# A decoder layer on eight cores: dealing out the query chunks evenly, and reworking how weights arrive before the first mixer

## The chip, the cores and the metric

One Trainium2 chip, all eight cores (dies: cores 0 to 3 and 4 to 7), one launch. The metric is device microseconds of the slowest core. On this chip an execution of such a program falls into one of two states: fast, where the granted TensorE clock averages about 0.96 to 0.98 on every core, or slow, where the cores of one die or both get less. "TensorE", "DVE", "ACT" and "Pool" are the matrix, vector, scalar and GpSimd engines; the rows of a profile name them PE (PEld for its weight loads), DVE, ACT and POOL, and SPq is the queue of plain DMAs.

## The reference, cut to what matters

```python
# x: (4, 4096, 2048); 8 heads of 128
h = rmsnorm(x)                       # then q, k, v, u, two gates = split(h @ w_in)
y_attn = stick_breaking_attention(q, k, v) @ w_attn_branch     # strictly causal
y_pool = (grouped(trailing_means(u, (2, 4, 8, 16)) - u) * pool_scale) @ w_pool_branch
x = x + rmsnorm((sigmoid(g_attn) * y_attn + sigmoid(g_pool) * y_pool) @ w_out)
up = causal_depthwise_conv(rmsnorm(x) @ w_up, width=3)         # 2 x 5632 channels
x = x + rmsnorm((gelu(gate) * val) @ w_down)
x = x + rmsnorm(sigmoid(x @ w_ple_gate) * (p @ w_ple))
```

Two cores share a sequence of 4096 tokens, that is 8 chunks of 512. Cores do not exchange anything: each makes keys and values for all chunks it attends to, and everything else for its own four chunks.

## The kernel before: the parts that matter

A core owned one half of a sequence. All eight run one program, so the program is the one of the second half, and cores with the first half ran it on zeros in front:

```python
xa = x[b] if half == 1 else np.concatenate([np.zeros((2048, D)), x[b, :2048]], axis=0)
...
groups = [(h, cc) for h in range(NH) for cc in range(c, -1, -1)]   # c = 4 + t, t = 0..3
```

So query chunk t goes over 5 + t key chunks. One step ("unit") takes 128 queries and 512 keys of one head: a score matmul, a sigmoid on ACT, a scan on DVE, four transposes, a copy on ACT, a weighted sum. Attention is interleaved with other TensorE work: the first one with the projections of chunks 5 to 7, the other three with mixers 0 to 2.

Weights come in float32. A DMA on the Pool queue can cast. Most units (0.5 MB in bf16) are first converted in DRAM, two at a time, and read from there through a ring of eight slots:

```python
def convert(u0, u1):                                  # float32 wst -> bf16 ws, DRAM to DRAM
    P.dma("pool", s_cv, [(ws[u0:u1]..., wst[u0:u1]...)], writes=[("ws", u0, u1)])
...
conv.extend(range(U_V, U_UP, 2))                      # 44 pairs: V, Q and all mixer weights
kst = [alloc(NT, BF16) for _ in range(3)]             # staging of K and Q on their way to DRAM
```

A helper works out, for every instruction, the semaphores it has to wait on; a conversion reads and writes DRAM only, so it waits for nothing but its place in the Pool queue.

## Time and profile before

| | before |
|---|---|
| four runs | 4899.15, 4901.73, 4919.94, 5198.72 us |
| profiled run, slowest core | 4903.9 us |
| TensorE busy | 4356.2 us (89%), union of matmul spans |
| start to first mixer | 1110 us |
| first to last mixer (attention beside) | 1326 us |
| last mixer, up, rest | 277, 647, 1544 us |

How to read it: from the first mixer on TensorE has little idle time, so there only a smaller count of matmuls helps. The first 1110 us are different. A busy total is not the amount of work: a 512-column matmul has a span of about 380 ns, but one can start every 215 ns.

### The profile page before, as it was taken

To read this page: it belongs to the slowest core of one execution; us is meant where nothing else is said; L and a number is where in the kernel's file an instruction comes from. 1 tells how busy PE (TensorE), PEld (TensorE's weight loads), DVE (VectorE), ACT (ScalarE), POOL (GpSimd) and SP (SyncE) were. 2 spreads that over 40 slices of the span, in tenths; PEclk is the share of its full clock that TensorE was granted. 3 is DMA by queue.
4 is the path that set the end of the run, shared out by engine and by line. 5 is a ranking of instruction groups with operands and counts; after the bars stand their busy time and mean duration, and the time that the engine had idled before them with its cause. 6 is when DMAs were issued, how large, how long until landed. Compare 5 with 4: busy or idle time off the path is not lost.

```text
span 4903.9 us, 73190 instructions; the slowest of 8 cores (4867.4 to 4903.9 us)
## 1 busy us (share of the span) xinstructions
PE 4356.2 (89%) x25253; PEld 2306.8 (47%) x25664; DVE 2274.5 (46%) x2149; ACT 1846.1 (38%) x3066; POOL 289.6 (6%) x652
## 2 busy tenths in 40 slices
PE   5896371899998999899799899999999999999988
PEld 2343130456864454455444566665444444444444
DVE  2221110696766887888531544442215444402244
ACT  2221010585555666666521333332003333301144
POOL 1000000000000000100000111110001111000000
PEclk9998685999999999999999999999999999999999
DMA  9799879554444544544553988886665444347643
GB/s 207 149 189 190 171 199 123 184 160 135 143 138 151 169 142 145 191 144 143 153 194 133 193 130 128 127 128 169 197 191 126 78 77 75 81 155 253 201 169 112
DMA packets 292253, 752.96 MB, mean 154 GB/s; under 512 B 61626, under 2 KB 174714, under 8 KB 270842
## 3 DMA queue, kind: packets, MB, share of 16 engines
q1 hardware_dynamic: 259396, 566.54, 36.2%
q0 software_dynamic: 32496, 181.72, 25.0%
q8 instruction: 213, 3.49, 0.3%
q14 instruction: 148, 1.21, 0.1%
HBM read 827.59 MB, written 171.44 MB: 204 GB/s over the span
## 4 chain that ended last, share of the span: by engine, by line
PE 75%; DMA 11%; SPq 4%; DVE 3%; issue 3%; another core or an unknown queue 2%; ACT 2%; POOL 0%; DVEq 0%; ACTq 0%; POOLq 0%
PE PS L463 30%; PE PS L1325 23%; PE PS L1376 11%; SPq L199 4%; PE PS L861 3%; PE PS L899 3%; PE PS L932 3%; DMA KS<-SB 2%; DMA SB<-DVS 2%; DMA X<-SB 2%; DMA SB<-xr 1%; DMA SB<-X 1%; DMA SB<-KS 1%; DVE SB L571 1%
## 5 line engine op out<-in xcount | busy, mean ns | idle before, releaser
L463 PE MATMUL PS<-SB 128*128 128x512 bf16 (+3 forms) x9426 | 2020.2, 360 | 131.7 <-DVE SB L486 70.8
L463 PEld LDWEIGHTS PS<-SB 128*128 128x128 bf16 x9656 | 893.9, 99 | 926.6 <-issue 191.3
L1325 PE MATMUL PS<-SB 128*128 128x342 bf16 (+1 forms) x6984 | 1224.7, 336 | 9.5 <-ACT SB L1342 6.4
L769 DVE TENSOR_TENSOR_SCAN SB<-SB 128x512 bf16<-128x512 f32 (+1 forms) x836 | 972.4, 1200 | 175.5 <-ACT SB L872 145.3
L482 ACT ACTIVATE SB<-PS 128x512 bf16<-128x512 bf16 (+3 forms) x1017 | 609.2, 604 | 1150.7 <-PE PS L463 524.9
L1325 PEld LDWEIGHTS PS<-SB 128*128 128x128 bf16 x7040 | 683.0, 97 | 550.0 <-issue 7.5
L1376 PE MATMUL PS<-SB 128*128 128x512 bf16 x2758 | 609.4, 380 | 12.3 <-DMA SB<-ws 8.8
L565 ACT ACTIVATE SB<-SB 128x512 bf16<-128x512 f32 (+3 forms) x245 | 216.7, 884 | 806.1 <-DVE SB L486 653.7
L1349 DVE SCALAR_TENSOR_TENSOR SB<-SB 128x1024 f32<-128x1024 f32 x176 | 226.1, 1285 | 601.0 <-ACT SB L1342 601.0
L486 DVE COPY SB<-PS 128x512 f32<-128x512 f32 (+3 forms) x197 | 135.1, 686 | 773.0 <-PE PS L1376 437.7
L872 ACT ACTIVATE SB<-PS 128x512 f32<-128x512 f32 (+1 forms) x832 | 476.2, 573 | 36.1 <-PE PS L861 20.9
L1376 PEld LDWEIGHTS PS<-SB 128*128 128x128 bf16 x2816 | 275.8, 98 | 344.2 <-issue 16.4
L1339 ACT ACTIVATE SB<-PS 128x1026 f32<-128x1026 f32 (+1 forms) x176 | 180.3, 1024 | 669.7 <-PE PS L1325 659.9
L486 DVE CAST SB<-PS 128x512 bf16<-128x512 f32 (+2 forms) x151 | 97.5, 651 | 553.6 <-PE PS L463 403.8
L899 PEld LDWEIGHTS PS<-SB 128*128 128x128 bf16 x3136 | 241.9, 98 | 177.1 <-issue 13.0
L861 PE MATMUL PS<-SB 128*128 128x512 bf16 (+3 forms) x820 | 301.0, 368 | 21.1 <-ACT SB L872 14.0
L899 PE MATMUL PS<-SB 128*128 128x128 bf16 x3136 | 312.0, 220 | 7.0 <-ACT SB L482 4.4
L932 PE MATMUL PS<-SB 128*128 128x512 bf16 (+3 forms) x907 | 292.5, 346 | 14.0 <-DMA SB<-DVS 6.6
L571 DVE SCALAR_TENSOR_TENSOR SB<-SB 128x2048 f32<-128x2048 f32 (+2 forms) x98 | 229.7, 2344 | 83.8 <-POOL SB L560 68.9
L1352 DVE SCALAR_TENSOR_TENSOR SB<-SB 128x1024 f32<-128x1024 f32 x176 | 226.2, 1285 | 18.7 <-DVE SB L1349 0.5
L1342 ACT ACTIVATE SB<-PS,SB 128x1026 f32<-128x1026 f32 (+1 forms) x176 | 212.3, 1206 | 37.9 <-DMA X<-SB 20.9
L586 PE MATMUL PS<-SB 128*128 128x128 bf16 x1024 | 81.9, 244 | 159.3 <-DVE SB L571 138.5
(53 smaller groups left out, 1322.6 us busy)
## 6 DMA issues: line engine op xcount, KB each, us to landing
SB<-ws SPq DMA_DIRECT2D x520, 512.0 KB, 3.9
SB<-wst POOLq DMA_DIRECT2D x192, 512.0 KB, 7.0
ws<-wst POOLq DMA_DIRECT2D x74, 1024.0 KB, 14.1
SB<-xr SPq DMA_DIRECT2D x48, 1024.0 KB, 12.2
SB<-X SPq DMA_DIRECT2D x36, 1024.0 KB, 9.1
X<-SB SPq DMA_DIRECT2D x32, 1024.0 KB, 7.4
SB<-KS SPq DMA_DIRECT2D x240, 128.0 KB, 3.1
SB<-DVS SPq DMA_DIRECT2D x240, 128.0 KB, 3.3
```

Source lines behind the costliest of these rows:

```text
L463: ins = e.matmul(o, l, r, start=(start and a + i == 0), stop=(a + i == n - 1), skip_group_check=True)
L482: P.op("act", lambda e: e.activation(out=dst, in_=src, func=AF.Copy), reads=reads, writes=writes)
L486: P.op("dve", lambda e: e.tensor_copy(dst, src), reads=reads, writes=writes)
L571: P.op("dve", lambda e: e.scalar_tensor_tensor(out=dst, in0=xv, scalar=cv, in1=gv, op0=ALU.mult, op1=ALU.mult), reads=[xr_, small.r(col, c ...
L769: P.op("dve", lambda e: e.tensor_tensor_scan(out=pb.v(lo, NT), data0=gb.v(lo, NT), data1=mask, initial=init, op0=ALU.mult, op1=ALU.max), r ...
L861: P.op("pe", lambda e: e.matmul(bank(bk, NT - lo, lo), q_.v(b_ * 128, (b_ + 1) * 128), kb_.v(lo, NT), start=True, stop=True), reads=[kb_.r ...
L872: P.op("act", lambda e: e.activation(out=gb.v(lo, NT), in_=bank(bk, NT - lo, lo), func=AF.Sigmoid, scale=-QSCALE), reads=[bkr(bk)], writes ...
L899: ins = e.transpose(at[:, q_ * 128:(q_ + 1) * 128], src[q_].v(kb * 128, (kb + 1) * 128), ident)
L932: ins = e.matmul(o_, l, r, start=(first and i == 0), stop=False, skip_group_check=True)
L1325: ins = e.matmul(bank(bs[bi], c1 - c0), w3[:, k, :], hT2v[:, k, c0:c1], start=(k == 0), stop=(k == 15), skip_group_check=True)
L1352: P.op("dve", lambda e, u_=u_, t_=t_, w0=w0: e.scalar_tensor_tensor(out=t_.v(0, 1024), in0=u_.v(2, 1026), scalar=w0, in1=t_.v(0, 1024), op ...
L1376: ins = e.matmul(bank(b), actb[kk].v(q_ * 512 + blk * 128, q_ * 512 + (blk + 1) * 128), w3[:, k, :], start=(kk == 0), stop=(kk == NF - 1), ...
```

## The change

Its intent: give each core an equal share of the causal triangle, and take load off the DMA engines in the start.

```diff
+OWN = ((0, 3, 4, 7), (1, 2, 5, 6))            # query chunks of the two cores of a sequence
+OTH = ((1, 2, 5, 6), (0, 3, 4, 7))
...
-groups = [(h, cc) for h in range(NH) for cc in range(c, -1, -1)]
+NK = 2 * t + 2
+groups = [(h, j) for h in range(NH) for j in range(NK)]
...
+def first_direct(u):                           # every second pair of mixer units
+    return U_U <= u < U_UP and (u - U_U) // 2 % 2 == 1
+if first_direct(u) and u not in was_direct:    # cast straight into the ring, write back later
+    P.dma("pool", s_ringd[s], [(ringb[s].v(), wst[u])], ...)
+    after(6000, lambda: P.dma("sp", s_back[s], [(ws[u], ringb[s].v())], ...))
...
 def convert(u0, u1):
-    P.dma(..., writes=[("ws", u0, u1)])
+    P.dma(..., writes=[("ws", u0, u1)], after=("pe", P.esem["pe"], P.cnt["pe"]))
-conv.extend(range(U_V, U_UP, 2))               # 44 pairs
+conv.extend(u for u in range(U_U, U_UP, 2) if not first_direct(u))    # 18 pairs
...
-kst = [alloc(NT, BF16) for _ in range(3)]
+kst = 4 buffers + 6 more                       # ten
+wv, wk, wq resident: each of 24 units loaded once with a cast
...
+merge(poses([5]), 16 * GRP, end[0])            # attention 0 beside chunk 5
+merge(poses([6, 7]), 32 * GRP, end[1])         # attention 1 beside chunks 6 and 7
```

(Cut: the order of the first loads; key addresses that depend on the core, chosen by a branch in the sync engine's program; chunks of zeros in front of chunk 0; edge tokens of two runs of chunks instead of one, in pooling, halo attention and convolution, all now done in the last mixer.)

## The prediction

> **What bounds the kernel now.** I read the page's 40 slices first, then busy time by stage, then the waits of TensorE, then single rows for prices. From the page:
>
> ```profile
> PE   5896371899998999899799899999999999999988
> ...
> DMA  9799879554444544544553988886665444347643
> ```
>
> One slice is 122.6 us. From slice 8 on TensorE is the bound; in the first seven it is not, and there the DMA engines are 80 to 99% busy. I cut the span where stages begin: 515 (keys, values, queries of the first five chunks of 512 tokens done), 1110 (first mixer), 2436 (last mixer, no attention beside it), 2713 (up-projection), 3360, 3672 (second up-projection), 4278. Columns: window, its length, busy us (count) of PE, PEld, DVE, ACT, POOL, granted clock, DMA share, GB/s.
>
> ```profile
> 0.00:515.00 515.00, 362.00 (x1963) 178.59 (x2000) 117.59 (x112) 105.56 (x128) 46.27 (x101) 0.89 0.92 185
> 515.00:1110.00 595.00, 384.32 (x2282) 191.08 (x2328) 236.07 (x228) 200.62 (x381) 14.60 (x32) 0.82 0.71 164
> 1110.00:2436.00 1326.00, 1253.67 (x8624) 728.48 (x8788) 1003.27 (x1017) 825.01 (x1660) 31.42 (x38) 0.99 0.47 151
> 2436.00:2713.00 277.00, 249.03 (x1197) 115.19 (x1222) 79.41 (x92) 50.75 (x89) 7.61 (x19) 0.95 0.51 169
> 2713.00:3360.00 647.00, 626.20 (x4294) 416.87 (x4294) 307.26 (x238) 249.14 (x233) 86.49 (x217) 0.98 0.84 136
> ...
> 3672.00:4278.00 606.00, 600.65 (x2742) 270.37 (x2797) 293.26 (x229) 235.80 (x223) 76.78 (x179) 1.00 0.47 88
> ```
>
> The first two rows are the loose ones: clock 0.89 and 0.82, PE busy 746 of 1110 us. TensorE's waits in 0 to 900 us (total, times, longest):
>
> ```profile
> PE PS L799 <- DMA SB<-KS: 118.8, 5, 101.8
> PE PS L586 <- DVE SB L571: 98.5, 10, 29.1
> PE PS L840 <- DMA SB<-DVS: 59.9, 10, 36.2
> PE PS L463 <- DVE SB L486: 59.5, 9, 33.7
> ```
>
> L799 and L840 are attention for two halo tokens, L586 the transposes of normed input, L463 the projections. L571 and L486 are themselves late because of an input load or because a staging buffer is still being stored: I take all four rows for DMA delay. The chain of waits names it, and the list of DMA issues and the queues name the culprit:
>
> ```profile
> 106.63 41.13 DMA KS<-SB
> ```
> ```profile
> ws<-wst POOLq DMA_DIRECT2D x74, 1024.0 KB, 14.1
> ```
> ```profile
> q0 software_dynamic: 32496, 181.72, 25.0%
> ```
>
> A 128 KB key store takes 41 us (median 7.3) because weight conversions (float32 to bf16, DRAM to DRAM) share the engines. Queue q0's 181.72 MB took 25.0% of 4904 us, or 6.75 us per MB, so a conversion of 1.05 MB holds all 16 engines for 7.1 us. 44 of the 74 (units 8 to 95) run before the mixers: 312 us of DMA.
>
> **What the Trainium skill says.** "DMA: Bandwidth & Descriptors", section "Issuing engines are not separate DMA queues": DMAs of all issuers interleave on the same 16 engines. The 41 us store agrees. "TensorE: Matmul & The Clock Gate", section "What's actually happening": the array is at half clock after idling until it has been busy for some 3.4 us. The trace agrees: after the 101.8 us wait weight loads come 0.43 us apart for about 5 us, then 0.22. Same page, "Back-to-back issue gap": N/2.4 + 2.5 ns, 216 ns for 512 columns. Agrees: 2816 matmuls in 606 us are 0.215 us each. "Perfetto Trace Analysis", section "Identifying the Most-Contended Engine": matmul busy time doesn't measure headroom. It agrees: those 2816 are each 378 ns long in the trace at that spacing of 215. So I price by counts and spacing, not by busy time.
>
> **Prices.** 512 columns 0.215 us; 128 columns 0.067 (16 transposes in 1.06 us); one projection group of 128 matmuls 27.5. A full attention unit (128 queries of one head by 512 keys: a score, a weighted sum, four transposes) 2 x 0.215 + 4 x 0.067 = 0.698; the 32 diagonal units of a query chunk together 16. DVE per full unit: one scan, 1.268 us.
>
> **The change, part by part.**
>
> (1) Query chunks are dealt out evenly. Before, a core had one half of the sequence and every core ran the schedule of the second half, on zeros in the first: 5, 6, 7, 8 key chunks. Now the two cores of a sequence own chunks (0,3,4,7) and (1,2,5,6): 2, 4, 6, 8. Full units fall from 704 to 512, at 0.698 us 134 us less. The order of instructions confirms: full scores 736 to 544, attention transposes 3136 to 2368, full scans 740 to 551. Keys and values are still made for all eight chunks.
>
> (2) K, V and Q weights stay resident, loaded once with a cast: 24 units at 0.52 MB x 6.75 = 3.5 us, 85 us of DMA. Conversions before the mixers fall from 44 to 18: 8 were for V and Q units, 18 go because every second pair of mixer units now comes by a casting load in the first mixer and is written back (36 x 3.5 us of DMA, in a stage where the engines are half free). Saved before the mixers: 26 x 7.1 = 184 us of DMA, plus 48 streamed V and Q units at about 1.6 us (0.52 MB at q1's 566.54 MB in 36.2% of the span, 3.1 us per MB), 79 us. Staging buffers for K and Q go from 3 to 10, and each conversion waits for TensorE's place in the program.
>
> (3) Costs. Two chunk edges instead of one: halo attention has 7 steps for 4 (+24 scores, +96 narrow matmuls, about 11 us), a block of edge rows (+32 matmuls, 7 us), the halo's mixer rows move from the first mixer to the last, 1026 columns become 1032 (4224 x 2/2.4 ns = 3.5 us).
>
> **Stage sums.**
>
> Start to first mixer, before: 20 groups 550, input transposes 34, first attention 128 x 0.698 + 16 = 105, halo 24: 713 us of TensorE, took 1110, so 397 lost. After, chunks 0 to 4: 14 groups 385, edge work 15, transposes 27 = 427. To it I add 40 us until the first projection (before: 49.77) and 30 for weights: by the time V starts some 23 MB must have landed, 115 us at the 200 GB/s of this stage, about when TensorE asks. 497 us. Chunks 5 to 7 with the first two attentions: 6 groups 165, transposes 9, attention 128 x 0.698 + 32 = 121, sum 295. But DVE then has 128 x 1.268 + 53 (diagonal) + 59 (evacuations, norms) = 274, ACT about 270. [...]I take 1.15, 340. Together 837, saving 273.
>
> Three mixers with attention, before: 3 x 260, + 24 halo, + 576 x 0.698 + 48 = 1254; took 1326, a factor of 1.058. After: 3 x 260 + 7, attention 384 x 0.698 + 32 = 300, halo 28: 1115 x 1.058 = 1179, + 10 for halo loads, which are prefetched only 2 to 3 deep against 3.1 us each: 1189. Saving 137.
>
> Last mixer: 277 + 17 (halo rows and narrower columns) + 20: the halo row's normalisation (two scalings and an addition of 2.3 us on DVE, a square sum of 1.9, the tiny Pool steps, transposes, edge copies) must now end before the up-projection starts: 314. First up-projection: 647 + 3.5, less some 10 as the other chains are spread out: 641. The rest, 3360 to 4904, is unchanged: 1544. Sum 837 + 1189 + 314 + 641 + 1544 = 4525; as my 1.15 is the cautious end, I say 4515.
>
> **Rivals.** *The start stays DMA-bound.* All eight cores still pull 24 float32 weight units and four input blocks at once; for it speaks the 0.99 DMA share of the first 60 us, against it the DMA sum of roughly 350 us for a 497 us stage. It would cost 60 to 100 us: about 4600. *DVE takes over.* With 274 of 295 us in the first two attentions, the scan chain could set the pace; against it, at 0.76 (1003 of 1326) it cost only 5.8%. If the merges of attention ran at 1.25: +30, about 4550. *The last mixer's halo chain or casting loads in the first mixer stall TensorE* (36 casting loads at 7.0 us to landing, eight slots): +20 to 40. *The start becomes wholly TensorE-bound*: losses of 50 instead of 115 us, about 4440. For nothing gained, the DMA hole would have to reappear in full (+270) and eat part of the attention's gain; even then about 4790 remain, more than 2% faster.
>
> **Range and chances.** Within the sum the start carries nearly all the doubt, -75 to +100. So 4420 to 4620 holds eight times in ten. Two independent gains, each over 2%, point the same way: faster 0.97, within 2% 0.02, slower 0.01.
>
> **What would show it.** Right: PE slices 2 to 7 at 8 or 9 with clock above 0.95 and the 100 us hole gone; first mixer starting at 800 to 880 us; last mixer starting near 2030; second up-projection unchanged at 606 us; 551 scans. Step (2) is wrong if TensorE's waits in the first 500 us on DMA-fed rows still exceed 100 us; the factor 1.15 is wrong if the two early attentions take over 370 us or under 310 with DVE busy; the halo step is wrong if TensorE idles over 30 us between last mixer and up-projection.

## The result, and the profile after

Of the 14 executions of the changed kernel six were fast, 4525.54 to 4542.29 us (median 4530); eight were slow, 4560.99 to 5239.02 us. Ten of the 14, five of them fast, ran in rounds with the kernel before. Their ratio is 0.9233, 95% interval 0.9215 to 0.9251: faster. A ratio is the mean time of one kernel's fast runs over that of the other's of the same rounds, so not quite the ratio of the medians quoted. Its own profile:

```profile
die 0 (median of its cores): 4704.4 us, clock 0.931
die 1 (median of its cores): 4569.1 us, clock 0.965
```

One die is 3% longer at a lower clock, so this profile is not compared. The kernel was run once more as a_same (below); those lines are from core 1 of that run, 4533.4 us. First the page's slices:

```profile
PE   5999888999889889998989999999999999998898
...
PEclk9999999999999899999999999999999999999999
DMA  9576656677665554447449997755664444356742
```

A slice is now 113 us. The 1 and the 3 of the first seven TensorE slices of before are gone, and after the first slice the DMA engines are 50 to 80% busy in the start. The stages, by the same cuts as before, with the start cut again where chunks 0 to 4 end:

```profile
0.00:477.00 477.00, 428.18 (x2343) 207.28 (x2344) 128.21 (x123) 110.38 (x138) 38.95 (x89) 0.99 0.74 186
477.00:839.00 362.00, 310.44 (x2035) 165.82 (x2034) 259.43 (x256) 221.01 (x434) 18.29 (x32) 0.94 0.59 150
839.00:2037.00 1198.00, 1113.23 (x6822) 564.07 (x6821) 738.58 (x733) 601.51 (x1174) 40.56 (x70) 0.98 0.61 180
2037.00:2356.00 319.00, 286.49 (x2168) 204.08 (x2168) 96.92 (x156) 63.41 (x142) 10.66 (x26) 0.95 0.55 168
2356.00:2978.00 622.00, 621.60 (x4290) 417.66 (x4291) 306.26 (x238) 248.86 (x231) 87.82 (x214) 1.00 0.87 139
2978.00:4533.00 1555.00, 1492.03 (x7039) 680.93 (x7037) 530.94 (x463) 415.99 (x576) 97.65 (x246) 0.98 0.53 145
```

| stage | before | predicted | measured |
|---|---|---|---|
| start, chunks 0 to 4 | | 497 | 477 |
| start, chunks 5 to 7 with attention | | 340 | 362 |
| start to first mixer | 1110 | 837 | 839 |
| three mixers with attention | 1326 | 1189 | 1198 |
| last mixer | 277 | 314 | 319 |
| first up-projection | 647 | 641 | 622 |
| rest | 1544 | 1544 | 1555 |
| sum | 4904 | 4525 | 4533 |

TensorE's longest waits in this run (total, times, longest):

```profile
PE PS L640 <- DVE SB L625: 47.4, 9, 23.7
PE PS L1000 <- DMA SB<-DVS: 33.3, 8, 12.6
PE PS L856 <- DMA SB<-KS: 26.9, 15, 7.3
...
PE PS L1254 <- DVE SB L625: 13.6, 1, 13.6
...
PE PS L898 <- DMA SB<-DVS: 13.0, 5, 6.2
```

L640 is the old L586 (input transposes); 45.0 of its 47.4 us fall in the first 120 us. L1000 is the weighted sum of full attention, L856 and L898 are scores and weighted sums of the halo tokens, L1254 is the halo row's transposes between last mixer and up-projection. The attention work shrank as counted (the DVE scans, first of the kernel before, then of this run):

```profile
L769 DVE TENSOR_TENSOR_SCAN SB<-SB 128x512 bf16<-128x512 f32 x740 | 912.6, 1268 | 156.9 <-ACT SB L872 132.5 <-PE PS L899 9.7 <-ACT SB L482 4.2
L824 DVE TENSOR_TENSOR_SCAN SB<-SB 128x512 bf16<-128x512 f32 x551 | 681.3, 1268 | 147.6 <-ACT SB L940 123.2 <-ACT SB L522 7.5 <-PE PS L929 6.1
```

There are 551 scans of 1268 ns, where before had 740 of the same length.

### The profile page after: what moved, and what is told of

Its sections match the earlier page's. It is cut to its first block, busy times and chain, and to the rows that moved or that the text cites. A ratio compares the mean times of both kernels' runs of the same rounds, so it can differ in the third digit from the quotient of the medians.

```text
span 4707.8 us, 69931 instructions; the slowest of 8 cores (4558.3 to 4707.8 us)
## 1 busy us (share of the span) xinstructions
PE 4455.4 (95%) x24692; PEld 2289.1 (49%) x24692; DVE 2061.0 (44%) x1966; ACT 1659.4 (35%) x2692; POOL 293.3 (6%) x677
## 4 chain that ended last, share of the span: by engine, by line
PE 87%; DMA 5%; DVE 2%; SPq 2%; issue 2%; ACT 1%; POOL 0%; ACTq 0%; DVEq 0%; POOLq 0%
PE PS L503 37%; PE PS L1495 28%; PE PS L1547 14%; PE PS L1000 3%; PE PS L967 2%; PE PS L929 2%; SPq L219 2%; DMA SB<-KS 1%; DMA SB<-DVS 1%; PE PS L640 1%; DMA SB<-xr 1%; DVE SB L625 1%; ACT SB L522 1%; DMA SB<-ws 1%; DVE SB L526 0%
## 5 line engine op out<-in xcount | busy, mean ns | idle before, releaser
L503 PEld LDWEIGHTS PS<-SB 128*128 128x128 bf16 (+1 forms) x9688 | 911.9, 100 | 898.8 <-issue 280.7
L1495 PE MATMUL PS<-SB 128*128 128x344 bf16 (+1 forms) x7040 | 1326.3, 355 | 7.2 <-ACT SB L1513 4.1
L1495 PEld LDWEIGHTS PS<-SB 128*128 128x128 bf16 x7040 | 712.5, 101 | 619.2 <-issue 331.9
L824 DVE TENSOR_TENSOR_SCAN SB<-SB 128x512 bf16<-128x512 f32 (+3 forms) x647 | 742.4, 1181 | 159.1 <-ACT SB L940 126.6
L522 ACT ACTIVATE SB<-PS 128x512 bf16<-128x512 bf16 (+4 forms) x830 | 498.2, 606 | 812.8 <-PE PS L503 299.3
L619 ACT ACTIVATE SB<-SB 128x512 bf16<-128x512 f32 (+2 forms) x246 | 218.6, 889 | 861.4 <-DVE SB L526 748.3
L1547 PEld LDWEIGHTS PS<-SB 128*128 128x128 bf16 x2816 | 291.1, 103 | 392.4 <-issue 228.0
L1511 ACT ACTIVATE SB<-PS 128x1032 f32<-128x1032 f32 (+1 forms) x176 | 180.7, 1027 | 782.4 <-PE PS L1495 771.5
L940 ACT ACTIVATE SB<-PS 128x512 f32<-128x512 f32 (+3 forms) x640 | 360.8, 565 | 22.3 <-PE PS L929 11.2
L625 DVE SCALAR_TENSOR_TENSOR SB<-SB 128x2048 bf16<-128x2048 f32 (+2 forms) x99 | 232.1, 2344 | 89.9 <-POOL SB L614 89.9
L1000 PE MATMUL PS<-SB 128*128 128x512 bf16 (+3 forms) x768 | 241.7, 343 | 25.5 <-DMA SB<-DVS 21.7
L967 PEld LDWEIGHTS PS<-SB 128*128 128x128 bf16 x2368 | 185.0, 99 | 128.9 <-issue 6.0
L1513 ACT ACTIVATE SB<-PS,SB 128x1032 f32<-128x1032 f32 (+1 forms) x176 | 212.6, 1208 | 38.3 <-DMA X<-SB 21.6
```

The lines of the kernel that those rows point to most:

```text
L503: ins = e.matmul(o, l, r, start=(start and a + i == 0), stop=(a + i == n - 1), skip_group_check=True)
L522: P.op("act", lambda e: e.activation(out=dst, in_=src, func=AF.Copy), reads=reads, writes=writes)
L625: P.op("dve", lambda e: e.scalar_tensor_tensor(out=dst, in0=xv, scalar=cv, in1=gv, op0=ALU.mult, op1=ALU.mult), reads=[xr_, small.r(col, c ...
L824: P.op("dve", lambda e: e.tensor_tensor_scan(out=pb.v(lo, NT), data0=gb.v(lo, NT), data1=mask, initial=init, op0=ALU.mult, op1=ALU.max), r ...
L940: P.op("act", lambda e: e.activation(out=gb.v(lo, NT), in_=bank(bk, NT - lo, lo), func=AF.Sigmoid, scale=-QSCALE), reads=[bkr(bk)], writes ...
L967: ins = e.transpose(at[:, q_ * 128:(q_ + 1) * 128], src[q_].v(kb * 128, (kb + 1) * 128), ident)
```

## The experiments

The theory: the gain is two gains, about 275 us in the start, because the DMA engines were overloaded, and about 135 us beside the mixers, because attention units went. Rivals for the start: conversions hurt by coming in bursts and not by their amount; the staging buffers; the streamed weights. Rivals inside my sum: the DVE scan as the pace of the early attention.

Differences in us below are taken against a_same, the changed kernel run once more, unless "before" is named. The runs were made in four sets, on chips 4, 7, 4 and 3, with the kernel before in each. The mean of its fast runs was 4907, 4923, 4923 and 4916 us, and a_same belongs to the third set. So a difference across sets carries up to some 16 us that are not the edit's; the ratios are free of that.

### b_gate: before, with the conversions' wait alone

```diff
-                  writes=[("ws", u0, u1)])
+                  writes=[("ws", u0, u1)], after=("pe", P.esem["pe"], P.cnt["pe"]))
```

> The kernel before with one thing of the change: each weight conversion waits until TensorE has reached the conversion's place in the program. Theory 'bursts' (conversions issued together starve the small loads; in the 101 us hole 12 of them hold 82.6% of the DMA engines and a key load takes 106 us to land): the hole goes, 80 to 160 us faster than before (ratio 0.967 to 0.984). Theory 'amount' (the 312 us of conversions are simply too much DMA before the mixers): within 1% of before, as nothing is taken away.

Fast runs 4832 to 4844 us, ratio 0.9861 (0.9845 to 0.9878): 70 us, a little under the "bursts" forecast. In before, the list of DMA queues and issues from 730 to 860 us, the hole, shows what a burst does:

```profile
q0 software_dynamic: 576, 12.58, 82.6%
...
ws<-wst POOLq DMA_DIRECT2D x12, 1024.0 KB, 65.1
...
SB<-KS SPq DMA_DIRECT2D x5, 128.0 KB, 106.3
```

Twelve conversions are issued in this stretch, eight of them together at 732.67 us and the rest as earlier ones land. They hold 82.6% of the engines; a 128 KB key load lands after 106 us. The 576 packets carry 12.58 MB, 22 KB each on average. The Trainium skill, "DMA: Bandwidth & Descriptors", section "Queues, rings and completion order", says that an engine switches between queue rows only at packet boundaries; that fits a small load crawling past 22 KB packets, though no run here varied the packet size. With the gate TensorE's wait of 101.8 us on such a load is gone, but only 70 us come out: the DMA work is the same, and other waits have grown (on value loads, L932, 29.3 us on the profiled core for 6.6 before).

### b_fewconv: before, with 36 of 44 early conversions left out

```diff
-conv.extend(range(U_V, U_UP, 2))
+conv.extend(range(U_V, U_U, 2))
...
+w = U_V + u % 16 if U_U <= u < U_UP else u        # mixers read V and Q units: wrong result
-P.dma("sp", s_ring[s], [(ringb[s].v(), ws[u])], ...)
+P.dma("sp", s_ring[s], [(ringb[s].v(), ws[w])], ...)
```

> The kernel before, where the mixers' weight loads read the 16 converted V and Q units instead of their own (wrong result on purpose, same loads), so 36 of the 44 early conversions go: 256 us of DMA. Theory 'amount' or 'bursts': the start up to the first mixer, 1110 us, shrinks by 200 to 290 (ratio 0.94 to 0.96). Rival (three staging buffers, streamed V and Q weights, the slow order of the first loads set the start): less than 100 us (ratio above 0.98).

Its output is wrong, which doesn't matter for the time. Fast runs 4695 to 4707 us, ratio 0.9581 (0.9564 to 0.9598): 205 us for 36 conversions, 5.7 us each, of the 7.1 us of DMA that I had worked out for one. So in the kernel before most of a conversion was on the path. The run does not part "amount" from "bursts": without conversions there are no bursts either.

### a_nogate: the changed kernel without that wait

```diff
-                  writes=[("ws", u0, u1)], after=("pe", P.esem["pe"], P.cnt["pe"]))
+                  writes=[("ws", u0, u1)])
```

> The changed kernel without the wait of conversions for TensorE. Theory 'bursts': its 18 early conversions run together soon after 190 us and starve the stores and loads there: 30 to 100 us slower than the changed kernel (ratio to before 0.930 to 0.944 against 0.9233). Theory 'amount': the same DMA work, within 15 us (0.920 to 0.927).

Fast runs 4513 to 4520 us, ratio 0.9204 (0.9185 to 0.9222), not slower at all. The gate is worth 70 us with 44 conversions (b_gate) and nothing with 18. So the gate is not what makes the changed kernel fast, once the conversions are few. Whether bursts were a part of what made the kernel before slow is another question; a_back3 bears on it.

### a_dummy26 and a_allconv: conversions put back into the changed kernel

a_dummy26 adds 26 conversions of units that nobody reads from there; a_allconv undoes the casting first loads, so that 18 more are needed:

```diff
 a_dummy26:
-conv.extend(need)                                  # 18
+conv.extend(need mixed evenly with 26 unread pairs)   # 44
-conv_every(28000)
+conv_every(11450)
 a_allconv:
 def first_direct(u):
-    return U_U <= u < U_UP and (u - U_U) // 2 % 2 == 1
+    return False
-conv_every(28000)
+conv_every(14000)
```

(Abridged: the run spells out the list of 44, and lets a needed pair be found out of its order.)

> The changed kernel with 26 more gated conversions before the first mixer that nobody reads (44 as before, paced at 11.45 us instead of 28), 184 us of DMA. Theory 'amount': DMA is again the bound in the start, 100 to 180 us slower than the changed kernel (ratio 0.944 to 0.960). Theory 'bursts': with a DMA share of 0.6 from 120 to 830 us there are some 280 us of slack, and spread conversions fit in: less than 40 us slower (below 0.932).

> The changed kernel with all 36 conversions of mixer weights before the first mixer again, paced at 14 us, and no casting first loads and write-backs. 18 more conversions are 128 us of DMA; 26 unread ones (184 us) cost 113 us, or 4.3 us each. Theory 'amount': 18 x 4.3 = 78 us slower in the start, less a little for the lighter first mixer: 55 to 80 us slower than the changed kernel (ratio to before 0.934 to 0.940). If the casting loads merely move the cost into the first mixer: within 15 us.

a_dummy26: its two fast runs took 4642 and 4652 us, 106 and 115 us over a_same (no interval, too few fast runs). It fits "amount"; the gated conversions did not vanish in the slack. a_allconv had no fast run. On the undisturbed die of its eight runs the longest core took 4585 to 4605 us, against 4539 and 4547 for the like die of a_same: 38 to 66 us, 51 between the middle values, about the low end of the forecast. The first mixer did not get shorter in exchange (391 us on core 7 from its first activation to that of the second mixer, 392 in a_same). The cost of a conversion is larger where there are more of them: about 3 us for each of 18, 4.1 to 4.4 for 26, 5.7 in the kernel before, where no gate held them.

### a_kst3: three staging buffers

```diff
+del kst[3:]
```

> The changed kernel with three staging buffers for K and Q, as before, in place of ten. Theory 'amount' (the conversions were the cause, the late stores only their effect): under 15 us slower than the changed kernel (ratio to before 0.9233 to 0.927). Rival 'staging': the deeper staging is what freed TensorE in the start, 40 us slower or more (0.931 and up).

Fast runs 4564 to 4589 us, ratio 0.9312 (0.9268 to 0.9356): 28 to 53 us, between the two forecasts. Staging has a share of its own, and a smaller one than the conversions; it falls in the first 300 us (TensorE is busy 220 us of them on core 1, for 254 in a_same).

### a_back3 and a_back4: the parts put back together

The single parts sum to about 115 to 150 us (106 to 115, + 28 to 53, - 20 for a_nogate), not to the 271 us of the start. So I put them back together: a_back3 is a_dummy26 without gate and with three buffers; a_back4 adds copies as large as the V and Q weights that before streamed in chunks 5 to 7.

```diff
+JK = scr("JK", [16, 128, 2048])
+def stream_again(p, u):                           # 16 copies in each of chunks 5, 6, 7
+    if p >= 5:
+        P.dma("sp", s_jk[u % 8], [(JK[u], ws[U_V + u])], ...)
```

> The changed kernel with three parts put back at once: 26 unread conversions, no gate on conversions, three staging buffers. If the parts only add: 113 + 33 - 15 = 131 us slower than the changed kernel, near 4665 us (ratio to before 0.949). If they bring each other about (conversions in bursts delay stores, three buffers pass the delay on to TensorE): 170 us or more, 4700 us and up (0.957 and up).

> As a_back3, and 48 plain copies of 0.5 MB beside chunks 5 to 7, as many bytes as the V and Q weights that the kernel before streamed there. By DMA time, 48 x 1.6 = 77 us more work in a stage that is then full: 40 to 80 us slower than a_back3. If streaming cost nothing by itself: within 15 us of it.

a_back3: 4739 to 4745 us, ratio 0.9645 (0.9591 to 0.97), 207 us over a_same. The step that the single parts missed is the gate: with the 70 us that it was worth beside 44 conversions (b_gate) in place of the -20, they sum to 204 to 238. Its trace has a burst again, seven conversions issued together at 831.87 us on core 1. So "bursts" is a part of the gain after all, of some 70 us by this sum. That is an estimate: the bursts may also act through the three buffers, and no run takes the gate alone from a_dummy26, which would have measured it. a_back4: 4810 to 4816 us, ratio 0.9786 (0.9731 to 0.984), 274 us. That is the whole gain of the start: with everything else of the change in place, its first mixer begins as late as before's (the first activation of the mixer after pooling at 1178.7 us on core 1, against 1154.7 before and 897.4 in the changed kernel; 1007.3 in a_dummy26, 1100.5 in a_back3). So the delay of these runs arises in the start. The longest waits of a_back4 in the first 1150 us, and its second window in the cut of before (core 1):

```profile
PE PS L1010 <- DMA SB<-DVS: 180.0, 13, 61.2
PE PS L642 <- DVE SB L627: 123.8, 15, 39.9
```
```profile
515.00:1110.00 595.00, 359.97 (x2229) 189.85 (x2230) 275.38 (x270) 230.49 (x442) 28.68 (x55) 0.80 0.93 182
```

DMA share 0.93 and clock 0.80, against before's 0.71 and 0.82 there. That fits parts that act through one shared thing, the time of the 16 DMA engines; it is argued from the traces, no run varies that time alone. One reservation: the copies go from DRAM to DRAM and not into SBUF, so the 67 us of a_back4 over a_back3 are an upper guess for streaming itself.

### a_padlate and a_padearly: the price of an attention unit

Both put 96 of the 192 removed full units back, over key chunks of zeros, which leave the result right.

```diff
-NPAD = 2
+NPAD = 3
-NK = 2 * t + 2
+NK = (2, 4, 8, 9)[t]        # a_padlate: beside the mixers
+NK = (4, 5, 6, 8)[t]        # a_padearly: beside chunks 5 to 7
```

> The changed kernel with 96 of the 192 removed full attention units put back, on key chunks of zeros (result stays right), all beside the mixers: third query chunk 8 key chunks for 6, fourth 9 for 8. Price of a unit there by the prediction, 0.698 us x 1.058: 71 us more (ratio 0.938). If the DVE scan of 1.268 us set the pace: 122 us (0.948). If attention hid behind the mixers' work: near 0.

> The same 96 units put back beside chunks 5 to 7 instead: first query chunk 4 key chunks for 2, second 5 for 4. Early stage bound by TensorE: 71 us as in the run with late padding (ratio 0.938). Bound by DVE, as the prediction's 274 of 295 us and the measured 358 us of the stage suggest: 96 x 1.268 = 122 us (0.948). Bound by DMA latency of the key and value loads: above 130 us.

a_padlate: 4601 to 4620 us but for one slow run, ratio 0.9367 (0.9329 to 0.9405). Its fast median of about 4611 is 75 us over a_same, or 0.78 us a unit, where 0.698 x 1.058 gives 0.74. Attention beside the mixers costs its TensorE time, so the 192 units are worth 142 to 150 us there. a_padearly: its one fast run took 4640 us, 104 us over, 1.08 us a unit: more than TensorE's price, less than the 1.268 us scan.

### a_early4 and a_dvdeep: what sets the pace of the early attention

a_early4 spreads the first two attentions over chunks 4 to 7, so that scans are thinner; a_dvdeep only loads attention's values four steps earlier, into the same buffers.

```diff
 a_early4:
-run(p0_pos(4)); merge(poses([5]), 16 * GRP, end[0]); merge(poses([6, 7]), 32 * GRP, end[1])
+merge(poses([4, 5, 6, 7]), 64 * GRP, end[1])      # attention starts 24 us of its clock later
 a_dvdeep:
-prefetch_dv((s - 4) // 4)
+prefetch_dv(s // 4)
```

> The changed kernel with the first two attentions spread over chunks 4 to 7 rather than 5 to 7. If the DVE scans set the pace of that stage (the 96 units put back cost 1.13 us each there, against 0.75 beside the mixers), spreading them gives 20 to 40 us (ratio to before 0.915 to 0.919). If latency of key and value loads or DMA load sets it: within 8 us of the changed kernel, or slower.

> The changed kernel with attention's value loads issued four steps earlier, the same four buffers. If late value loads set the pace of the first two attentions (33 us of TensorE waits on them there): 15 to 33 us faster than the changed kernel (ratio to before 0.915 to 0.919). If the DVE scans do: within 8 us, as other waits take their place.

a_early4: 4522 to 4527 us, ratio 0.9191 (0.9147 to 0.9236), 11 us better than a_same's median, less than "scan" asked for; the intervals overlap. a_dvdeep: 4512 to 4519 us, ratio 0.9192 (0.9154 to 0.9229), 18 us better, as the "late values" theory said, though again the intervals overlap. The trace carries it further: TensorE's waits of 33 us on value loads (SB<-DVS) leave the list, and in the window of 477 to 839 us DVE got more work done in the same time. First the top of TensorE's waits from 400 to 950 us in a_dvdeep (core 1):

```profile
PE PS L929 <- DMA SB<-KS: 14.9, 3, 11.3
PE PS L929 <- ACT SB L940: 8.5, 16, 1.4
```
Then the row of its window from 477 to 839 us (columns as in the stages above: span, busy time of PE, PEld, DVE, ACT and POOL, clock, DMA share, GB/s):

```profile
477.00:839.00 362.00, 327.09 (x2177) 174.82 (x2176) 279.24 (x275) 234.93 (x463) 19.34 (x34) 0.97 0.62 158
```

In the first, a wait on key loads takes half the place of the one removed. The second is to be held against the changed kernel's row for the same window: PE 327 against 310, DVE 279 against 259. An engine that had been the bound could not have gained work from an earlier load.

### a_haloring: deeper loads for the halo tokens

```diff
+kr5, dvr6 = both(kr, qr), both(dvr, vsr)          # borrow the idle query and value buffers
-ldk = lambda j, h: load(kr, ...);  lddv = lambda j, h: load(dvr, ...)
+ldk = lambda j, h: load(kr5, ...); lddv = lambda j, h: load(dvr6, ...)
```

> The changed kernel where the halo attention loads its keys through five buffers and its values through six, borrowing the idle query and value buffers, instead of three and four. If the prefetch depth makes TensorE wait (44 us of waits on those loads in the trace, where the prediction had 10): 25 to 44 us faster than the changed kernel (ratio to before 0.914 to 0.918). If the waits come from loads queued behind weight loads on the same DMA engines: within 8 us.

Fast runs 4512 to 4523 us, ratio 0.9177 with a wide interval (0.9116 to 0.9237): near 20 us. On core 1 the last mixer starts 18.6 us earlier, all of it after the first mixer. The halo waits fall from 39.9 us to 25.4, so depth is a part; the rest stays.

```profile
PE PS L862 <- DMA SB<-KS: 16.9, 5, 8.8
...
PE PS L904 <- DMA SB<-DVS: 8.5, 2, 4.3
```

### a_same, a_best and a_best2: the changed kernel again, and better versions

> The changed kernel itself once more, to have it beside the next three and with a profile in the fast state: ratio to before 0.921 to 0.926, 4525 to 4545 us, first mixer starting near 830 us, last near 2020.

> Both remedies, the deeper halo loads and the attention spread over chunks 4 to 7. The sum of the single gains: 15 to 60 us faster than the changed kernel (ratio to before 0.911 to 0.920).

> Deeper halo loads, attention spread over chunks 4 to 7 and earlier value loads together. a_best stood at 4496 us (ratio 0.914); the earlier loads add 0 to 25 us: 4470 to 4496 us (ratio 0.909 to 0.915).

a_same: fast runs 4536, 4536 and 4540 us, ratio 0.922 (0.9176 to 0.9263), which agrees with the first result. a_best (deeper halo loads, attention over chunks 4 to 7): 4497 to 4501 us, ratio 0.914 (0.9097 to 0.9183). a_best2 (and earlier value loads): 4480 to 4486 us, ratio 0.9119 (0.9093 to 0.9145), correct. It beats both kernels, the changed one by 1.2% (0.9119 against 0.9233, intervals apart).

## Why the prediction was right or wrong

**The amount, in the fast state: right.** 4515 was forecast, 4530 is the fast median. Both gains are there in the sizes given: 271 us in the start (273 forecast), 128 us beside the mixers (137 forecast). The experiments put the first on how weights and stores load the DMA engines (a_back4 restores 274 us of it) and the second on TensorE's work (a_padlate, 0.78 us a unit for 0.74). That the start came within 2 us is partly luck: its two stages were 20 us shorter and 22 us longer than forecast, and the 10 us that were taken off the sum because 1.15 was "the cautious end" were taken off for a factor that proved too small.

**The step that failed: "Range and chances".** The prediction wrote that "the start carries nearly all the doubt" and named 4420 to 4620 us for eight runs in ten. It said nothing of the slow state, although one of the four times given for before, 5198.72, showed it. Of the 14 executions recorded with the result, six lie above 4620, the highest at 5239. Before fared no better: eight of its 15 runs there were slow, and its median over all of them is 5089.9 us. From that median the ratio gives 5089.9 x 0.9233 = 4700 us, outside the range. The doubt about the sum was far smaller than stated (every fast run within 0.7% of 4515), the doubt about the state was left out. What puts an execution into the slow state stays open: no run here shows it. A range has to name the state it is for, or be given for the ratio.

**Part (2), the conversions: right in kind, but other parts weigh as much.** The prediction named 26 conversions and 48 streamed units, 263 us of DMA, and credited the start with 273. The 273 did not come from these 263: it is what was left of 1110 us after TensorE's counted work and an allowance. Conversions alone are 106 to 115 us (a_dummy26), about two fifths, staging 28 to 53, and the lack of the gate some 70 by the sum under a_back3; the 67 us of a_back4 over a_back3 are at most the streamed weights'. The gate, which the prediction mentions without a price, thus weighs about as much as the streaming that it priced at 79.

**Chunks 0 to 4, 497 us: 20 too long.** Of the 70 us added to TensorE's 427 (40 until the first projection, 30 for weights) 50 were needed: the first projection starts at 46 us on core 1, and after the first 120 us the stage has next to no waits (2.4 us).

**The factor 1.15 for the early attention: too small, and for the wrong reason.** 362 us were measured for 295 of TensorE work, 1.23. I put it down to DVE at 274 of 295 us. DVE was busy 259 of 362 us, and the value loads, one group ahead of use, made TensorE wait 33 us; loading them earlier came out about 18 us faster, in medians whose intervals overlap. The rival "DVE takes over" was not it, and late loads in that stage were not among the rivals. The rest of the excess stays unexplained.

**10 us for halo loads: four times too small.** 39.9 us were measured. I had the depth and the latency but let most of it hide.

**The last mixer: right.** 319 us for 314; the halo row's chain stands as one wait of 13.6 us and one of 3.0.

**First up-projection, 641 us: 19 too long.** The stalls there are gone (waits of 16.6 us on the input transposes and 4.1 us on ACT before), and its matmuls keep TensorE busy for 618.5 of 622 us. The prediction took off 10 us for this; no run shows that the spreading of other chains did it.

**Rivals.** "The start stays DMA-bound" did not happen, and a_back3 and a_back4 show what it would have looked like. "Casting loads in the first mixer stall TensorE" did not: a_allconv, without them, has no shorter first mixer.

**A slip in the working.** "The start becomes wholly TensorE-bound" takes 65 us off (losses of 50 for 115), which gives 4450 to 4460 and not 4440.

## What to carry to other kernels

Where the DMA engines are full, price parts by their share of DMA time, and test them put back together before crediting or dismissing one: the gate was worth nothing beside 18 conversions and 70 us beside 44. Count work at issue spacing, by stage, and give each stage its own bound: that sum held to 0.3% here, though two of its reasons were wrong and two of its errors cancelled.

## What the Trainium skill lacked or had wrong

- "TensorE: Matmul & The Clock Gate", section "Back-to-back issue gap": it gives a sustained 131 ns per 512-column matmul in a stream of weight loads and matmuls. Here such streams run at 0.215 us (2816 in 606 us), which is the page's isolated formula; no stage of these runs comes near the lower figure.
- Same page, section "Seeing it yourself": it says to budget 13/16 of the clock for dense work on all cores. In the fast profile of a_same all eight cores average 0.976 to 0.980, and the stage of 2816 in 606 us, in before, ran at 1.00, so the limit did not hold in them. The lowest means of slow runs are 0.80 to 0.82, near its 81.2%. Why one execution falls to it and another of the same kernel does not is on no page, and no run here shows it.
- "DMA: Bandwidth & Descriptors": it has no price for a casting copy. In the kernel before, the Pool queue, nearly all float32 to bf16 copies, took 6.75 us of all 16 engines per MB written, the plain DMAs 3.1 us.
- Same page: that queues share engines packet by packet is there, but not what it does to small loads. Beside large casting copies with packets of 22 KB, twelve issued within 50 us, 128 KB loads took 106 us to land, against a median of 3.1.
